# A decoder trunk on one core: the first MLP pair of a block multiplies both input parts in one 512-column matmul, background jobs pause for the residual, two sigmoids move behind an attention split

## The chip, the cores and the metric

The kernel runs on one core of a Trainium2 chip. The metric is the device time of one execution in microseconds (us). Three runs of the kernel before took 1474.15 us in the median (1473.31 to 1476.63). One further execution was profiled.

The engines are written as the profile writes them: PE is the matmul engine, PEld its weight loads, DVE the vector engine, ACT the scalar engine, POOL the GpSimd engine, SP the queue that issues most loads. Each engine works through its own instructions in order.

## The reference, cut to what matters

Two layers on a sequence of 512 tokens, model width 1024, MLP width 4096, all in 32-bit floats:

```python
h = rmsnorm(x, g_mix);  z = h @ w_in            # q, k, v, retention q, k, v, g, two gates
ya = sliding_window_sink_attention(aq, ak, av, sinks) @ w_a
r = chunkwise_retention(rq, rk, rv)             # then a group norm
r = r * rsqrt(mean(r * r) + EPS) * silu(rg);  yb = r @ w_b
x = x + (sigmoid(ga) * ya + sigmoid(gb) * yb) @ w_out
h2 = rmsnorm(x, g_mlp)
x = x + square(relu(h2 @ w_up)) @ w_down        # the MLP
# after both layers: rmsnorm(x, g_final)
```

## The kernel before, in words

**Numbers.** Every operand of a product is split into two parts of a narrower format, high and low: `hi` and `lo` for weights, `xh` and `xl` for inputs. A product is then three matmuls that add up in the same PSUM bank: high by high, high weights by the low input part, low weights by the high input part. The helper `products` (L387 to L396) issues them, on lines L394, L395 and L396. Weights arrive by DMA as tiles of 128 x 1024 called `raw`; `split_until` rounds one on ACT into `hi` (L342) and subtracts on DVE for `lo` (L343), up to three units ahead of PE. `split` (L417, L418) does the same for inputs.

**The MLP.** The 4096 columns of `w_up` go through in eight blocks of 512 a layer. From the second block on (e = 1 to 7) the up-projection of a block is done as two pairs of 256 columns each, by a scheme with seven instead of eight products of half size: tokens in two halves of 256 (`H`), model width in two halves of 512. The sums of inputs that the scheme needs are formed once a layer in `Forms`; the sums of weights are formed in DRAM by background jobs and added on DVE (L283, L306, L322). In `pair` the seven products run as `multiply` calls into three PSUM banks a, e, b; each call takes 4 steps of 128 rows, three matmuls of 256 columns a step. Results are copied or added out of PSUM by ACT and DVE (L1526 to L1546). The first pair of a block hands its result z to `first_two` (or, in the last block of the last layer, `first_plain`), which squares and splits it; the second pair feeds z in pieces to `second`, `second_late` and `second_rest`. `down` then multiplies the squared result by a block of `w_down` in the same scheme: seven `multiply` calls of 12 matmuls with 512 columns. Results go out by POOL DMAs that add into `y` in DRAM (L1674). The framework's scheduler orders instructions across these functions by its own simulated times, so matmuls of `down`, of the first pair and of the second pair interleave on PE.

**Background jobs.** `sum_steps` forms the sums of weights in DRAM: for each job a copying DMA and an accumulating one, both on POOL's queue (L231, L234), the accumulating one behind the copy. In layer 0 there are 27 jobs and a last sum called `sums_last` (L242, L244, L245), so 29 steps; in layer 1 there are 26 jobs and 27 steps. Nothing runs them but calls of `pace(src)`: every second call puts a one-column copy on POOL (L259, `mark`), which waits for `src`, and issues the next step behind it. While `quiet[0]` is set, `pace` does nothing.

**Before the output projection.** The residual x has to leave its place on chip for the gated mixture, which is formed in the same tile (`mixed`). After `w_b` the mixture is turned into input sums on DVE (`ms.first`, `ms.second`, `ms.third`; L1251 to L1267) and split; then POOL loads the residual back, slice by slice (L1307), and the projection `output()` adds its products to it on DVE (L1373 and L1374).

**The retention gate.** `silu(i)` takes a sigmoid on ACT (L1062) and multiplies on DVE (L1063). The first four run after the last exponential of the attention; the last attention output is split on ACT and DVE (L417, L418, into `last_split`), and PE needs that split for `w_a`.

Of the kernel before, what the change touches and what calls it, by code (L numbers as in the profile page):

```python
# [11 lines left out]
F32R = mybir.dt.float32r  # L12
# [104 lines left out]
def decoder(ctx, tc, xT, x_first, w_in, w_rg, w_rv, w_a, w_b, w_wo, w_up, w_pair, w_down, w_end, tables, decay, band, g_last, out):  # L117
# [29 lines left out]
    sink = little_x[:, P - n_gain - n_sink : P - n_gain]  # L147
    eps, half, nsink = (little_x[:, a : a + n] for a, n in ((0, 1), (8, N_KV), (16, n_sink)))
    x = little_x[:, P:].rearrange("p (k t) -> p k t", t=T)
    xh = const.tile([P, KD, T], F32R, name="xh")  # L150
    xl = const.tile([P, KD, T], F32R, name="xl")
    late = ctx.enter_context(tc.tile_pool(name="late", bufs=1))

    def late_tile(dtype):
# [302 lines left out]
    def group(name, layer, moving, evacuates, meanwhile=None, low_last=None):  # L457


        banks = [bank(ps_mm, "mm") for _ in range(4)]  # L460
        for u in range(4):
            with ExitStack() as queue:
                if low_last:
                    state["hold"] = state["next"] + 2 if u < 2 else None
                for ins in behind.pop(0) if behind else ():
                    queue.enter_context(tc.issue_after(ins))
                hi, lo = unit(name, layer)
            if low_last:
                by_halves(
                    banks,  # L470
                    (hi, lo),
                    moving,
                    (2 * u, 2 * u + 1),
                    lambda j, c: slice(j * T + c * P, j * T + (c + 1) * P),
                    low_last.get(u),
                )
            for j in range(0 if low_last else 2):
                advance()
                k = 2 * u + j
                for c, ps in enumerate(banks):  # L480
# [25 lines left out]
    class Forms:  # L506


        def __init__(self, ks):
            self.parts, self.own = {}, []  # L510
            self.tiles = {}
            for k in ks:
                self.tiles[k] = []
                for _ in range(2):
                    t, own = slots.four()
                    self.own.extend(own)
                    self.tiles[k].append([t[:, 2 * i : 2 * i + 2, :].rearrange("p a (b t) -> p (a b) t", t=H) for i in range(2)])

# [3 lines left out]
        def keep(self, ks, first, f, js):  # L522
            hi, lo = self.tiles[ks][first // 2]
            at = slice(2 * (js[0] - first), 2 * (js[-1] - first) + 2)
            split(hi[:, at, :], lo[:, at, :], f[:, at, :])
            for j in js:
                for i in range(2):
                    self.parts[j, ks + i] = tuple(t[:, 2 * (j - first) + i, :] for t in (hi, lo))

        def one(self, ks, b):  # L530
            self.f = [big("sums").rearrange("p a (b t) -> p (a b) t", t=H) for _ in range(2)]
# [89 lines left out]
    def layer_body(layer):  # L621
# [554 lines left out]
        with tc.issue_after(last_exp[0]):  # L1176
            for hs in (slice(0, T // 2), slice(T // 2, T)):
                nc.scalar.activation(x[:, :, hs], x[:, :, hs], AF.Sigmoid)
            for i in range(4):
                silu(i)  # L1180
        turned.take()
        quiet[0] = True
# [43 lines left out]
        class Mixed:  # L1226
# [63 lines left out]

        rT.extend(tuple(view(s) for s in ret[k]) for k in range(4))
        group("w_b", layer, rT, [put_mixed(c) for c in range(4)], {1: second_pair})
        for c in range(6, KD):
            gate_tile(c)
            chunk("w_in", layer, xs, gate(gates[c]))
        for c in range(4, KD):
            quiet[0] = c > 5
            chunk("w_b", layer, rT, put_mixed(c))
        quiet[0] = False
        for k in range(KD):  # L1300
# [181 lines left out]
        def second_late(z):  # L1482
            second(z, TWO, LATE)
            if not kept:
                return
            u_forms.middle(0, kept[0], z, (1,))
            u_forms.keep(0, 2, u_forms.f[1], (2,))

        def second_rest(z):
            if not kept:  # L1490
                return
            kept.pop()
            u_forms.rest(0, z, (3,))
# [15 lines left out]

            return put  # L1510

        def pair(which):
            def multiply(ps, weights, left, moving, start=True):
                hi, lo = weights
                cols = [slice((0 if left else 4 * P) + k * P, (0 if left else 4 * P) + (k + 1) * P) for k in range(4)]
                products(ps, [((hi[:, c], lo[:, c]), m) for c, m in zip(cols, moving)], start, True, not start)

            a, e, b = (bank(ps_mm, "mm")[:, :H] for _ in range(3))
            eu, z = temp("eu"), big("z")
            part = unit("pair", layer)
            multiply(a, part, True, block(0, 0))
            nc.scalar.activation(b, a, AF.Copy)  # L1526
            multiply(e, part, False, sums[0])
            nc.scalar.activation(eu[:, :H], e, AF.Copy)
# [5 lines left out]
            if which:  # L1534
                second(z, slice(0, 1), SOON)
            part = unit("pair", layer)
            multiply(b, part, True, sums[2], False)
            nc.vector.scalar_tensor_tensor(z[:, 1, H:], b, -1.0, eu[:, :H], ALU.mult, ALU.subtract)
            multiply(e, part, False, block(1, 1), False)
            nc.vector.tensor_tensor(z[:, 0, H:], e, eu[:, H:], ALU.add)  # L1540
            nc.scalar.activation(z[:, :, H:], z[:, :, H:], AF.Relu)
            if which:
                second_late(z)
            part = unit("pair", layer)
            multiply(b, part, True, sums[3], False)
            nc.scalar.activation(z[:, 1, :H], b, AF.Relu, scale=-1.0)  # L1546
            if which:
                second(z, slice(1, 2), SOON)
                second_rest(z)
            elif plain:  # L1550
                first_plain(z)
            else:
                first_two(z)

        def down_plain(into):
            sums.free()
# [245 lines left out]
        for e in range(N_BLOCK):  # L1802
            if e == 0:
                into = Adding(e)
                hooks = first_hooks()
                for c in (0, 2):
                    two_chunks("w_up", layer, xs, [put_up(c), put_up(c + 1)], hooks[c // 2])
            else:
                plain = last and e == N_BLOCK - 1
                into = Ending() if e == N_BLOCK - 1 else Adding(e)  # L1810
                if last and e == 2:
                    with tc.issue_after(state["high"]):
                        nc.scalar.activation(sq[:, 0:1], factor[:, 0:1], AF.Sqrt)
                pair(0)
                pair(1)
            if last and e == N_BLOCK - 1:
                down_plain(into)
            else:
                down(e, into, None if e else lambda: rest.append(sum_input(2)))
                if e == 0:  # L1820
                    rest.pop()()
# [185 lines left out]
```

## Time and profile before

| What | Value |
|---|---|
| Median of three runs | 1474.15 us |
| The profiled execution, its own time | 1475.95 us |
| Its span, first to last instruction | 1473.9 us |
| PE busy | 1451.4 us (98%) |
| DVE busy | 1181.1 us (80%) |
| ACT busy | 974.5 us (66%) |
| POOL busy | 229.7 us (16%) |
| Mean granted PE clock | 0.997 |

The profile shows one execution. Rows of the timeline give the start, the duration, the engine, the line and operation, the tile written and those read, the shape, a count where equal instructions are merged, and in brackets the idle time before and who ended it. Matmuls overlap in the pipeline, so the duration of one is longer than the distance to the next. "A <- B: 7.0, 1, 7.0" in the list of waits means that A waited for B for 7.0 us in all, once, and 7.0 us at the longest.

### The profile page before, as it was taken

To read this page: it belongs to the slowest core of one execution; us is meant where nothing else is said; L and a number is where in the kernel's file an instruction comes from. 1 tells how busy PE (TensorE), PEld (TensorE's weight loads), DVE (VectorE), ACT (ScalarE), POOL (GpSimd) and SP (SyncE) were. 2 spreads that over 40 slices of the span, in tenths; PEclk is the share of its full clock that TensorE was granted. 3 is DMA by queue.
4 is the path that set the end of the run, shared out by engine and by line. 5 is a ranking of instruction groups with operands and counts; after the bars stand their busy time and mean duration, and the time that the engine had idled before them with its cause. 6 is when DMAs were issued, how large, how long until landed. Compare 5 with 4: busy or idle time off the path is not lost.

```text
span 1473.9 us, 22472 instructions
## 1 busy us (share of the span) xinstructions
PE 1451.4 (98%) x8185; PEld 1271.8 (86%) x8185; DVE 1181.1 (80%) x1776; ACT 974.5 (66%) x1590; POOL 229.7 (16%) x335
## 2 busy tenths in 40 slices
PE   9999999999899999999999999999999999999998
PEld 7888888888888999999888888888889889999997
DVE  6977877868698888888779788878689888888885
ACT  6656655544487777787656576556447877777775
POOL 0011002321101111111200110022211111111120
PEclk9999999999999999999999999999999999999999
DMA  7598249999735766666964983499975477777664
GB/s 258 180 292 235 90 141 301 285 281 263 201 113 186 182 176 178 180 182 184 313 195 150 288 260 104 151 306 259 280 187 185 154 196 194 191 195 190 175 187 149
DMA packets 97295, 302.83 MB, mean 205 GB/s; under 512 B 11425, under 2 KB 11553, under 8 KB 90785
## 3 DMA queue, kind: packets, MB, share of 16 engines
q0 software_dynamic: 36512, 129.78, 37.5%
q1 hardware_dynamic: 59952, 170.32, 33.9%
q8 instruction: 64, 1.05, 0.3%
q10 hardware_dynamic: 720, 1.31, 0.2%
q14 instruction: 47, 0.38, 0.1%
HBM read 261.78 MB, written 120.06 MB: 259 GB/s over the span
## 4 chain that ended last, share of the span: by engine, by line
PE 90%; DMA 3%; issue 3%; DVE 2%; ACT 1%; POOL 1%; DVEq 0%; POOLq 0%; ACTq 0%
PE mm L395 21%; PE mm L396 21%; PE mm L394 21%; PE wo L1351 4%; PE rg L1015 3%; PE b L394 3%; PE b L395 3%; PE b L396 3%; PE rv L395 2%; PE rv L394 2%; PE rv L396 2%; PE mm L410 2%; DMA sums_up<-w_pair_in 1%; PE score L780 1%; PE pT L745 1%
## 5 line engine op out<-in xcount | busy, mean ns | idle before, releaser
L342 ACT ACTIVATE hi<-raw 128x1024 fp32r<-128x1024 f32 (+1 forms) x393 | 400.1, 1022 | 255.1 <-PE mm L395 120.0
L343 DVE TENSOR_TENSOR lo<-raw,hi 128x1024 fp32r<-128x1024 f32 (+1 forms) x394 | 458.9, 1174 | 93.7 <-ACT hi L342 90.7
L394 PE MATMUL mm<-xh,hi 128*128 128x512 f32 (+1 forms) x912 | 319.1, 354 | 1.7 <-DVE rot L642 0.6
L395 PE MATMUL mm<-xl,hi 128*128 128x512 f32 (+1 forms) x912 | 319.6, 353 | 0.0
L396 PE MATMUL mm<-xh,lo 128*128 128x512 f32 (+1 forms) x912 | 316.2, 353 | 0.1
L394 PEld LDWEIGHTS mm<-xh,hi 128*128 128x128 f32 x912 | 173.2, 190 | 25.7 <-ACT xh L420 1.3
L395 PEld LDWEIGHTS mm<-xl,hi 128*128 128x128 f32 x912 | 173.3, 190 | 21.9
L396 PEld LDWEIGHTS mm<-xh,lo 128*128 128x128 f32 x912 | 172.2, 190 | 21.5 <-DVE lo L343 0.3
L395 PE MATMUL mm<-r,hi 128*128 128x256 f32 (+1 forms) x608 | 189.3, 311 | 0.5 <-DVE r L418 0.5
L394 PE MATMUL mm<-r,hi 128*128 128x256 f32 (+1 forms) x608 | 186.2, 312 | 3.4 <-ACT r L417 2.9
L396 PE MATMUL mm<-r,lo 128*128 128x256 f32 (+1 forms) x608 | 189.0, 311 | 0.0
L394 PEld LDWEIGHTS mm<-r,hi 128*128 128x128 f32 x608 | 115.5, 190 | 12.8 <-ACT r L417 4.0
L395 PEld LDWEIGHTS mm<-r,hi 128*128 128x128 f32 x608 | 115.8, 190 | 9.4 <-DVE r L418 1.4
L396 PEld LDWEIGHTS mm<-r,lo 128*128 128x128 f32 x608 | 115.8, 190 | 6.3
L1674 POOL DMA_DIRECT2D y<-eu x56 | 63.0, 1401 | 372.0 <-DVE eu L1659 371.9
L395 PE MATMUL mm<-lo,r 128*128 128x512 f32 (+1 forms) x276 | 104.3, 387 | 0.0
L396 PE MATMUL mm<-hi,r 128*128 128x512 f32 (+1 forms) x276 | 100.9, 387 | 0.0
L394 PE MATMUL mm<-hi,r 128*128 128x512 f32 (+1 forms) x276 | 98.3, 389 | 0.3 <-ACT r L417 0.2
L394 PE MATMUL b<-hi,r 128*128 128x512 f32 x180 | 70.6, 392 | 1.9 <-DVE eu L1659 1.9
L1351 PE MATMUL wo<-r,hi 128*128 128x256 f32 x384 | 71.0, 287 | 0.0
L283 DVE TENSOR_TENSOR raw<-raw 128x512 f32<-128x512 f32 x56 | 38.5, 687 | 40.5 <-DMA raw<-w_pair_in 32.4
L395 PE MATMUL b<-lo,r 128*128 128x512 f32 x180 | 70.2, 390 | 0.0
(337 smaller groups left out, 2873.0 us busy)
## 6 DMA issues: line engine op xcount, KB each, us to landing
raw<-w_in_in SPq DMA_DIRECT2D x65, 512.0 KB, 5.5
sums_down<-w_down_in POOLq DMA_DIRECT2D x30, 1024.0 KB, 12.8
sums_up<-w_pair_in POOLq DMA_DIRECT2D x56, 512.0 KB, 12.1
raw<-w_down_in SPq DMA_DIRECT2D x45, 512.0 KB, 7.4
raw<-w_pair_in SPq DMA_DIRECT2D x84, 256.0 KB, 3.7
y<-y POOLq DMA_DIRECT2D x62, 256.0 KB, 9.7
y<-eu POOLq DMA_DIRECT2D x61, 256.0 KB, 8.5
raw<-sums_down SPq DMA_DIRECT2D x30, 512.0 KB, 7.2
```

What stands on the lines that cost most here:

```text
L283: nc.vector.tensor_tensor(raws[i][:, at], last[:, LEFT], last[:, RIGHT], ALU.add)
L342: state["high"] = nc.scalar.activation(hi[:, at], raw[:, at], AF.Copy).ins
L343: nc.vector.tensor_tensor(lo[:, at], raw[:, at], f32(hi[:, at]), ALU.subtract)
L394: nc.tensor.matmul(ps, ah, bh, start=start and i == 0, stop=False, **more)
L395: nc.tensor.matmul(ps, ah, bl, start=False, stop=False, **more)
L396: latest[0] = nc.tensor.matmul(ps, al, bh, start=False, stop=stop and i == n - 1, **more).ins
L410: latest[0] = nc.tensor.matmul(ps, w[:, cols(j, c)], moving[k][low], start=first, stop=bool(final)).ins
L745: nc.tensor.transpose(pt[:, i * P : (i + 1) * P], sm[:, at : at + P], ident)
L780: nc.tensor.matmul(ps[:, g * w : (g + 1) * w], q_s[g][:, c, at], part[:, keys], start=i == 0, stop=i == 1)
L1015: nc.tensor.matmul(o, w[:, cols], v, start=start and k == 0 and n == 0 and w is hi and v is vh, stop=k == 3 and n == 1 and w is lo, skip_g ...
L1351: latest[0] = nc.tensor.matmul(o, w[:, cols], v, start=start and first and n % 2 == 0 and w is hi and v is vh, stop=final and w is lo, ski ...
L1674: nc.gpsimd.dma_start(y[:, 2 * j + m, i * T : (i + 1) * T], t, **how)
```

## The change

Three edits.

1. `xh` and `xl` become two halves of one tile `x_both`, and `Forms` also keeps views that hold the high and the low part of a sum together. A new function `wide_pair` does the first pair of each block from e = 1 on: in each step the high weights multiply both input parts in one matmul of 512 columns (two pieces of 256), into both halves of a PSUM bank, and the low weights multiply the high part, 256 columns, into the first half. The halves are added on the way out: by an ACT copy of the first and a DVE operation that adds the second (`joined`), or by two DVE operations. The copy from a to b takes both halves. `pair` keeps the old form and now serves the second pair alone.
2. `quiet[0]` is set before the last two gate chunks (c = 6, 7) instead of in the middle of the last four `w_b` chunks, so that four more calls of `pace` do nothing.
3. `silu(2)` and `silu(3)` are issued after both halves of the last attention split.

```diff
-    xh = const.tile([P, KD, T], F32R, name="xh")
-    xl = const.tile([P, KD, T], F32R, name="xl")
+    x_both = const.tile([P, 2, KD, T], F32R, name="xs")
+    xh, xl = x_both[:, 0], x_both[:, 1]
...
+                    self.both[k].append(t.rearrange("p (c a) (b t) -> p c (a b) t", c=2, t=H))
...
+                    self.wide[j, ks + i] = self.both[ks][first // 2][:, :, 2 * (j - first) + i, :]
...
-            for i in range(4):
+            for i in range(2):
+                silu(i)
+        with tc.issue_after(last_split[0]), tc.issue_after(last_split[1]):
+            for i in range(2, 4):
                 silu(i)
...
+        quiet[0] = True
         for c in range(6, KD):
             gate_tile(c)
             chunk("w_in", layer, xs, gate(gates[c]))
         for c in range(4, KD):
-            quiet[0] = c > 5
             chunk("w_b", layer, rT, put_mixed(c))
         quiet[0] = False
...
+        def wide_pair():
+            def multiply(ps, weights, left, moving, start=True):
+                hi, lo = weights
+                for k, both in enumerate(moving):
+                    at = (0 if left else 4 * P) + k * P
+                    more = {"skip_group_check": True}
+                    nc.tensor.matmul(halves_of(ps), hi[:, at : at + P], both, start=start and k == 0, stop=False, **more)
+                    latest[0] = nc.tensor.matmul(
+                        ps[:, :H], lo[:, at : at + P], both[:, 0, :], start=False, stop=k == 3, **more
+                    ).ins
...
+            def joined(dest, ps, sign=1):
+                nc.scalar.activation(dest, ps[:, :H], AF.Copy, scale=float(sign))
+                nc.vector.scalar_tensor_tensor(dest, ps[:, H:], float(sign), dest, ALU.mult, ALU.add)
+
+            a, e, b = (bank(ps_mm, "mm") for _ in range(3))
+            eu, z = temp("eu"), big("z")
+            part = unit("pair", layer)
+            multiply(a, part, True, quarter_of(0, 0))
+            nc.scalar.activation(b, a, AF.Copy)
+            multiply(e, part, False, form(0))
+            joined(eu[:, :H], e)
+            part = unit("pair", layer)
+            multiply(b, part, True, form(1), False)
+            joined(eu[:, H:], b)
+            multiply(a, part, False, quarter_of(1, 0), False)
+            joined(z[:, 0, :H], a)
+            part = unit("pair", layer)
+            multiply(b, part, True, form(2), False)
+            nc.vector.scalar_tensor_tensor(z[:, 1, H:], b[:, :H], -1.0, eu[:, :H], ALU.mult, ALU.subtract)
+            nc.vector.tensor_tensor(z[:, 1, H:], z[:, 1, H:], b[:, H:], ALU.subtract)
+            multiply(e, part, False, quarter_of(1, 1), False)
+            nc.vector.tensor_tensor(z[:, 0, H:], e[:, :H], eu[:, H:], ALU.add)
+            nc.vector.tensor_tensor(z[:, 0, H:], z[:, 0, H:], e[:, H:], ALU.add)
+            nc.scalar.activation(z[:, :, H:], z[:, :, H:], AF.Relu)
+            part = unit("pair", layer)
+            multiply(b, part, True, form(3), False)
+            joined(z[:, 1, :H], b, -1)
+            nc.scalar.activation(z[:, :, :H], z[:, :, :H], AF.Relu)
+            if plain:
+                first_plain(z)
+            else:
+                first_two(z)
...
-                pair(0)
-                pair(1)
+                wide_pair()
+                pair()
```

More of the change, by code (lines that the diff above doesn't have):

```diff
@@ L510, in __init__ @@
             self.parts, self.own = {}, []
-            self.tiles = {}
+            self.tiles, self.wide, self.both = {}, {}, {}
             for k in ks:
-                self.tiles[k] = []
+                self.tiles[k], self.both[k] = [], []
                 for _ in range(2):
                     t, own = slots.four()
+                    self.both[k].append(t.rearrange("p (c a) (b t) -> p c (a b) t", c=2, t=H))
                     self.own.extend(own)
@@ L1510, in put_up, with halves_of, quarter_of, form @@
             return put
-        def pair(which):
+        def wide_pair():
[8 more added lines that the diff above has]
+                    ).ins
+            def halves_of(ps):
+                return ps.rearrange("p (a t) -> p a t", t=H)
+            def quarter_of(half, tokens):
+                at = slice(tokens * H, tokens * H + H)
+                return [x_both[:, :, k, at] for k in range(4 * half, 4 * half + 4)]
+            def form(j):
+                return [sums.wide[k] for k in sorted(sums.wide) if k[0] == j]
+            def joined(dest, ps, sign=1):
[29 more added lines that the diff above has]
+                first_two(z)
@@ L1513, in multiply, with pair @@
+        def pair():
             def multiply(ps, weights, left, moving, start=True):
@@ L1533, in pair @@
             nc.scalar.activation(z[:, 0, :H], a, AF.Relu)
-            if which:
-                second(z, slice(0, 1), SOON)
+            second(z, slice(0, 1), SOON)
             part = unit("pair", layer)
@@ L1541, in pair @@
             nc.scalar.activation(z[:, :, H:], z[:, :, H:], AF.Relu)
-            if which:
-                second_late(z)
+            second_late(z)
             part = unit("pair", layer)
@@ L1546, in pair @@
             nc.scalar.activation(z[:, 1, :H], b, AF.Relu, scale=-1.0)
[L1547 to L1553, printed above, removed]
+            second(z, slice(1, 2), SOON)
+            second_rest(z)
         def down_plain(into):
```

## The prediction

> **What bounds the kernel now.** I read the page first, then who PE waits for, then three stretches of the timeline.
>
> ```profile
> span 1473.9 us, 22472 instructions
> PE 1451.4 (98%) x8185; PEld 1271.8 (86%) x8185; DVE 1181.1 (80%) x1776; ACT 974.5 (66%) x1590; POOL 229.7 (16%) x335
> ```
>
> PE is busy for 1451.4 of 1473.9 us, so time can come from two places only: fewer or cheaper matmuls, or the 22.5 us in which PE stands. The waits of PE say where it stands:
>
> ```profile
> PE wo L1351 <- DVE lo L343: 7.0, 1, 7.0
> PE mm L394 <- ACT r L417: 3.0, 3, 1.7
> ```
>
> One hole of 7.0 us in the output projection, and short waits of 3.0 us in all behind an attention split. The windows put them beside a steady block of the MLP (columns: stretch, its length, busy us and count of PE, PEld, DVE, ACT, POOL, then PEclk, DMA share, GB/s):
>
> ```profile
> 143.00:182.00 39.00, 37.52 (x192) 31.73 (x191) 33.45 (x46) 23.82 (x34) 1.10 (x2) 1.00 0.30 98
> 380.00:394.00 14.00, 7.30 (x61) 7.10 (x60) 2.30 (x3) 2.72 (x4) 4.08 (x7) 0.93 0.71 188
> 394.00:417.00 23.00, 22.49 (x169) 22.23 (x170) 22.02 (x29) 16.18 (x25) 1.07 (x2) 0.89 0.57 185
> 595.80:635.00 39.20, 39.20 (x253) 35.85 (x252) 32.33 (x42) 30.28 (x50) 7.02 (x8) 1.00 0.70 185
> ```
>
> An MLP block has PE at 39.20 of 39.20, and DVE at 32.33. The change touches all three kinds of place.
>
> **Part 1, the wide pair.** A pair has 7 multiplies of 4 steps, each step three matmuls over 256 columns: 84 matmuls. In the first pair of each of the 14 blocks a step becomes one matmul of 512 and one of 256 columns. What PE pays is the distance between starts, not the duration shown:
>
> ```profile
> 612.12 0.39 PE L394 MATMUL b<-hi,r 128*128 128x512 f32 x1
> ...
> 614.84 0.28 PE L394 MATMUL mm<-xh,hi 128*128 128x256 f32 x1
> ...
> 616.27 0.40 PE L394 MATMUL b<-hi,r 128*128 128x512 f32 x1
> ```
>
> Twelve 512-column matmuls fill 612.12 to 614.84, 226.7 ns each; twelve of 256 fill 614.84 to 616.27, 119.2 ns each. A block is 168 x 119.2 + 84 x 226.7 ns = 39.07 us, against 39.20 in the window, so the two prices carry the stage. A step falls from 3 x 119.2 = 357.6 to 226.7 + 119.2 = 345.9 ns: 11.7 ns. There are 28 steps a pair and 14 pairs: 392 x 11.7 ns = 4.6 us. No row shows a moving operand in two pieces of 256 columns that lie apart. Its bounds: no gain, if each piece costs what a matmul of 256 costs (2 x 119.2 = 238.4 ns, as now); 4.6 us, if it costs what a 512-column row costs. A loss is excluded as long as one instruction with one weight load is not dearer than the two it replaces. I take 4.6: within a piece the columns lie side by side, as in the 512-column rows, and doubling the columns there costs 107.5 ns where a matmul of 256 costs 119.2, so 11.7 ns belong to the instruction and not to the columns.
>
> The Trainium skill ("TensorE: Matmul & The Clock Gate", section "Back-to-back issue gap") gives an isolated gap of N/2.4 + 2.5 ns, 109 and 216 ns here; by it a step would gain 2.6 ns and the part 1.0 us instead of 4.6. The trace disagrees with these gaps by about 10 ns a matmul (119.2 and 226.7), and the page itself says that a stream with a weight load before each matmul is not set by that formula.
>
> What the pair adds lies on ACT and DVE:
>
> ```profile
> L1538 DVE SCALAR_TENSOR_TENSOR z<-mm,eu 128x256 f32<-128x256 f32 x28 | 11.8, 420 | 10.1 <-PE mm L396 10.1
> L1612 ACT ACTIVATE b<-mm 128x512 f32<-128x512 f32 x30 | 17.5, 584 | 4.8 <-PE mm L396 4.8
> L1541 ACT ACTIVATE z<-z 128x512 f32<-128x512 f32 x28 | 17.3, 619 | 0.6 <-DVE z L1540 0.6
> 629.76 0.37 ACT L1546 ACTIVATE z<-mm 128x256 f32<-128x256 f32 x1
> ```
>
> DVE had 2 evacuations, now 8: six more of 0.42, 2.5 us a block; 32.33 becomes 34.8 of 38.9 us, still with room. ACT: the copy of a to b grows from 0.37 to 0.58, and one more Relu over 512 costs 0.62: 0.8 us on 30.28. I cost both at nothing, since PE is what these engines wait for in this stage (the L1538 row: 10.1 us idle before it, all on PE). If that cover is gone, it is 2.5 us a block, 35 us in all.
>
> The order matters more than the sums. The result of the first pair now goes Copy, DVE add, Relu, where it was one Relu: later by 0.42 + (0.62 - 0.37) = 0.7 us and a hand-over. Who waits for it is the next block-product:
>
> ```profile
> 632.33 0.62 ACT L417 ACTIVATE r<-z 128x512 fp32r<-128x512 f32 x1
> 633.34 0.69 DVE L418 TENSOR_TENSOR r<-z,r 128x512 fp32r<-128x512 f32 x1
> 634.85 0.63 PE L394 MATMUL mm<-hi,r 128*128 128x512 f32 x2
> 636.74 0.40 PE L395 MATMUL mm<-lo,r 128*128 128x512 f32 x1
> ```
>
> The high part is ready at 632.95 and used at 634.85, the low at 634.03 and used at 636.74: 1.9 and 2.7 us of room for about 1 us. It holds. Bank b is tighter: it is written again one multiply (4 x 345.9 ns = 1.4 us) after ACT and DVE start to read it; that is the slower rival below.
>
> **Part 2, the pause.** The hole, followed on PE, DVE, POOL and in the chain of work:
>
> ```profile
> 394.35 0.58 PE L1351 MATMUL wo<-r,lo 128*128 128x256 f32 x1 [7.05 <-DVE lo L343]
> ...
> 398.57 0.58 PE L1351 MATMUL wo<-r,hi 128*128 128x256 f32 x2
> ```
> ```profile
> 362.11 0.68 DVE L1267 SCALAR_TENSOR_TENSOR x<-x 128x512 f32<-128x512 f32 x1
> 377.75 0.68 DVE L1267 SCALAR_TENSOR_TENSOR x<-x 128x512 f32<-128x512 f32 x1
> 392.47 0.69 DVE L1373 TENSOR_TENSOR x<-x,kept 128x512 f32<-128x512 f32 x1 [11.70 <-DMA x<-xT_in]
> ```
> ```profile
> 360.02 0.83 POOL L234 DMA_DIRECT2D sums_down<-w_down_in  x1 [4.53 <-DMA sums_down<-w_down_in]
> 360.56 0.60 POOL L259 COPY mark<-gb 128x1 f32<-128x1 f32 x1
> 370.69 1.08 POOL L244 DMA_DIRECT2D sums_last<-sums_down  x1 [9.53 <-issue]
> 381.48 0.83 POOL L245 DMA_DIRECT2D sums_last<-w_down_in  x1 [9.72 <-DMA sums_last<-sums_down]
> 382.12 3.44 POOL L1307 DMA_DIRECT2D x<-xT_in  x6
> ```
> ```profile
> 383.77 8.62 DMA x<-xT_in
> ```
>
> POOL issues in order. The mark from gate chunk 7 (L259 at 360.56) sets off the last job step, two accumulating DMAs that each wait for the one before, and the loads of x stand behind them until 382.12. DVE then waits 11.70 us for x, the weight split L343 stands behind that, and PE 7.05 us behind the split. PE restarts slowly too: 19 matmuls from 394.35 to 398.57 take 4.22 us where 119.2 ns each make 2.26, so 1.96 more (the clock column reads 0.93 and 0.89). The hole costs 9.0 us.
>
> Counting calls of pace in layer 0 (8 in attention, 8 and 6 for the gates, 2 and 4 in qk, 8 in values, 16 in retention, 4 in the group): 56 before gate chunk 6, so 28 steps; the list needs 29. The pause takes away the four calls of chunks 6 and 7 and of two w_b chunks, and with them exactly that last step, which comes two calls later, in the projection's own put, after the loads of x. Then POOL is free from about 361, the first two slices of x go when L1267 at 362.11 has ended and the others from 378.4, when the second L1267 has. With the 8.62 us that such a load took, the slices for the first L1373 are there before 375, those for the second at 387 at the latest; it ran 4.6 us after the first, at about 385. A wait of 2 us there is inside the room DVE has: PE lost only 7.05 of DVE's 11.70. The last step lands later, but nothing queued on POOL wants to go until the first y store:
>
> ```profile
> 454.75 1.11 POOL L1674 DMA_DIRECT2D y<-y  x2 [58.40 <-ACT y L1669]
> ```
>
> I take 9.0; it is 5 if the second pair of slices comes late enough to hold DVE. Layer 1 has no such wait in the list, and its 27 steps end before the pause: nothing there.
>
> **Part 3, two sigmoids.** In both layers PE waits for the last attention split:
>
> ```profile
> 148.57 1.15 ACT L1062 ACTIVATE sig<-z 128x512 f32<-128x512 f32 x2
> 149.74 0.60 ACT L638 ACTIVATE rot<-mm 64x512 f32<-64x512 f32 x1
> ```
> ```profile
> 152.60 1.19 PE L394 MATMUL mm<-r,hi 128*128 128x512 f32 x4 [1.21 <-ACT r L417]
> 154.06 0.50 PE L395 MATMUL mm<-r,hi 128*128 128x512 f32 x1 [0.27 <-DVE r L418]
> ```
>
> The two sigmoids, 1.15 us, stand on ACT ahead of the split; behind it, the split comes 1.15 us sooner, and so does PE until it meets the low half on DVE. Bounds: 0, if another wait takes over, and 1.21 + 0.27 = 1.5 a layer. I take 1.0, as the low half has its own queue: 2.0 us in all. Queued behind the moved sigmoids on ACT is the preparation of the turned inputs (L895), and behind their two products on DVE its subtractions. PE wants these only after w_a and the first gate product; where they come too late for it, part 3 falls towards its lower bound.
>
> **The sum.** 4.6 + 9.0 + 2.0 = 15.6 us off the profiled execution's own time, 1475.95 us (its span is 1473.9, 2.05 less): 1460.35. The median of the runs, 1474.15, is 1.8 below that execution, so 1458.6 is what I predict.
>
> **Rivals.** (A) The wide matmul brings nothing, because the two pieces are read as two: parts 2 and 3 remain, 11.0 us, 1463.2. For it: no row shows such an operand. Against: the 11.7 ns that two matmuls of 256 cost more than one of 512. By the isolated gap of that page of the Trainium skill it would be 1462, nearly this case. (B) The pause does not fill the hole, as the later slices of x, freed only at 378.4, are late by their 8.62 us and hold DVE: part 2 is worth 5, or, with the throttled restart kept, 3; 1463 to 1465. This is the case in which the change does not do what it says. For it: 387 against 385. Against: PE's 4.6 us of room. (C) Slower: bank b. After its second and third product ACT (0.37) and DVE (0.42) must both have read it, and each may first have to finish a split already begun:
>
> ```profile
> L343 DVE TENSOR_TENSOR lo<-raw,hi 128x1024 fp32r<-128x1024 f32 x360 | 436.6, 1220 | 77.6 <-ACT hi L342 74.6 <-PE mm L395 1.5
> L342 ACT ACTIVATE hi<-raw 128x1024 fp32r<-128x1024 f32 x360 | 379.4, 1058 | 243.8 <-PE mm L395 119.5 <-issue 22.0 <-PE rv L396 21.4
> ```
>
> 0.37 + 0.42 + 1.06 + 1.22 = 3.1 us against the 1.4 us of the multiply between, a stall of 1.7 a block, 24 us in 14 blocks: 1482 after the gains. It decides from 15.6/14 = 1.1 us a block; at just that, the result is no change. Against it: matmuls of other products stand between in the trace (b forms between two multiplies at 616.27), and ACT and DVE idle for PE here, not PE for them.
>
> **How the numbers follow.** Forecast 0.66, (A) 0.13, (B) 0.07, (C) in full 0.10, a stall that just cancels the gains 0.04. The forecast's own spread is 1455 (both bounds of part 3, every end at its best: 4.6 + 9.0 + 3.0, and 2 us for the run) to 1463; A and B reach 1467 with a little more lost. So 1455 to 1467 leaves out C, the cancelling case and little else. Faster by over 0.2% (3 us, about what a measurement of this kernel can tell): 0.86; within: 0.04; slower: 0.10.
>
> **What would show it.** Right: a block of about 38.9 us with PE at 100%; matmuls of 512 in the first pair 227 ns apart from the next; no wait of wo L1351 on DVE, L1307 ahead of L244, no PEclk below 1.0 there; the wait on ACT r L417 near zero in both layers. Wrong: new waits of PE on ACT or DVE evacuations inside the MLP blocks, blocks of 40 us or more, or a hole that merely moved behind L1373.

## The result, and the profile after

The changed kernel takes 1517.8 us (median of 4 runs, 1517.37 to 1518.16) against 1474.44 us of the kernel before (4 runs beside it). The ratio is 1.0292, 95% interval 1.0274 to 1.031: slower by 43 us, where 16 us less was forecast. The profiled execution took 1518.16 us, its span is 1516.4 us.

The page first: the span, and busy time, share and instructions of each engine.

```profile
span 1516.4 us, 21805 instructions
PE 1461.0 (96%) x7793; PEld 1251.3 (83%) x7793; DVE 1210.9 (80%) x1860; ACT 980.0 (65%) x1604; POOL 227.2 (15%) x335
```

PE issues 392 matmuls fewer (7793 against 8185), exactly one a step, and yet is busy longer, and it stands for 55.4 us where it stood for 22.5. The waits of PE (total, times, longest) name the places:

```profile
PE mm L394 <- ACT r L417: 21.2, 14, 2.7
PE mm L1523 <- DVE eu L1540: 13.8, 12, 1.2
PE mm L396 <- DVE lo L343: 4.0, 2, 3.7
PE ret L394 <- DVE whole L770: 1.9, 1, 1.9
```

Two waits stand in nearly every MLP block. The 7.0 us of the output projection are gone. The windows of the changed kernel, in the columns of the prediction's windows; the last row is three blocks:

```profile
380.00:394.00 14.00, 14.00 (x119) 14.00 (x118) 11.87 (x15) 6.73 (x8) 3.17 (x4) 1.00 0.91 289
394.00:417.00 23.00, 22.84 (x142) 20.46 (x141) 22.14 (x34) 19.91 (x33) 0.83 (x1) 1.00 0.74 192
510.54:638.51 127.97, 120.28 (x672) 103.32 (x672) 102.86 (x142) 92.47 (x151) 21.06 (x24) 1.00 0.66 173
```

A block is 127.97/3 = 42.66 us long, 3.4 more than the 39.2 of before, and no engine is full in it: PE is busy for 40.1 us, DVE for 34.3, ACT for 30.8. That every engine has idle time points to the hand-overs between them rather than to a load; the experiments test it. Fourteen blocks of 3.4 would make 48 us; the output projection gives 9 back.

**The first wait, once a block.** The timeline of PE, ACT and DVE around it:

```profile
591.20 0.28 PE L1524 MATMUL mm<-r,lo 128*128 128x256 f32 x1
...
594.92 0.28 PE L396 MATMUL mm<-xs,lo 128*128 128x256 f32 x1
596.52 0.50 PE L394 MATMUL mm<-hi,r 128*128 128x512 f32 x1 [1.33 <-ACT r L417]
596.86 0.39 PE L395 MATMUL mm<-lo,r 128*128 128x512 f32 x1
...
591.40 1.06 ACT L342 ACTIVATE hi<-raw 128x1024 fp32r<-128x1024 f32 x1 [1.38 <-PE mm L1523]
592.37 0.37 ACT L1539 ACTIVATE z<-mm 128x256 f32<-128x256 f32 x1
...
594.09 0.63 ACT L1565 ACTIVATE z<-z 128x512 f32<-128x512 f32 x1 [0.41 <-DVE z L1540]
594.75 1.06 ACT L1471 ACTIVATE z<-z 128x1024 f32<-128x1024 f32 x1
595.84 0.63 ACT L417 ACTIVATE r<-z 128x512 fp32r<-128x512 f32 x1
...
592.49 1.23 DVE L343 TENSOR_TENSOR lo<-raw,hi 128x1024 fp32r<-128x1024 f32 x1 [2.29 <-ACT hi L342]
593.64 0.42 DVE L1540 SCALAR_TENSOR_TENSOR z<-mm,z 128x256 f32<-128x256 f32 x1
```

The last product of the first pair ends on PE with the L1524 of 591.20. Its result is copied by ACT only at 592.37, behind a weight split begun just before; DVE adds the second half only at 593.64, behind the other half of that split; then come Relu, Square and the split into r. PE gets r 5.2 us after its next matmul could start (591.32 to 596.52). It has 31 matmuls of the second pair to do meanwhile, to 595.04, and then stands.

**The second wait, once a block.** The same three engines, 28 us later:

```profile
621.57 0.40 PE L394 MATMUL b<-hi,r 128*128 128x512 f32 x1
...
623.21 0.28 PE L1524 MATMUL mm<-xs,lo 128*128 128x256 f32 x1
624.65 0.50 PE L1523 MATMUL mm<-xs,hi 128*128 128x512 f32 x1 [1.16 <-DVE eu L1540]
...
623.17 0.69 ACT L1721 ACTIVATE y<-b,columns 128x512 f32<-128x512 f32 x1 [3.35 <-PE b L396]
623.76 0.38 ACT L1539 ACTIVATE eu<-mm 128x256 f32<-128x256 f32 x1
...
624.17 0.42 DVE L1540 SCALAR_TENSOR_TENSOR eu<-mm,eu 128x256 f32<-128x256 f32 x1 [3.62 <-ACT eu L1539]
```

PE wants to write bank e again at 623.33, and e has been complete since 619.1. But its copy to eu (L1539) stands on ACT behind the evacuation of the block-product before (L1721), ACT has stood idle for 3.35 us for that one, and the six matmuls that L1721 waits for begin on PE only at 621.57, put by the scheduler between the third and the fourth step of the pair's fourth product. So PE waits for DVE, DVE for ACT, and ACT for matmuls that PE itself took late.

**The other two parts** did their work. POOL and DVE in layer 0 of the changed kernel:

```profile
362.46 1.16 POOL L1312 DMA_DIRECT2D x<-xT_in  x2 [8.15 <-DVE r L418]
...
380.38 1.06 POOL L1312 DMA_DIRECT2D x<-xT_in  x2 [2.41 <-DVE r L418]
...
389.31 1.11 POOL L244 DMA_DIRECT2D sums_last<-sums_down  x1
...
377.66 0.69 DVE L1378 TENSOR_TENSOR x<-x,kept 128x512 f32<-128x512 f32 x1
```

The loads of x go ahead of the last job step, DVE takes x at 377.66 without a wait (at 392.47 after 11.70 us before), and PE is full from 380 to 394 at a granted clock of 1.00.

### The profile page after: what moved, and what is told of

It reads as the page before. It is cut to its first block, busy times and chain, and to the rows that moved or that the text cites. A ratio compares the mean times of both kernels' runs of the same rounds, so it can differ in the third digit from the quotient of the medians.

```text
span 1516.4 us, 21805 instructions
## 1 busy us (share of the span) xinstructions
PE 1461.0 (96%) x7793; PEld 1251.3 (83%) x7793; DVE 1210.9 (80%) x1860; ACT 980.0 (65%) x1604; POOL 227.2 (15%) x335
## 4 chain that ended last, share of the span: by engine, by line
PE 88%; ACT 5%; issue 3%; DVE 3%; DMA 1%; ACTq 0%; DVEq 0%
PE mm L394 18%; PE mm L395 18%; PE mm L396 17%; PE mm L1523 6%; PE wo L1356 5%; PE mm L1524 3%; PE rg L1017 3%; PE b L394 2%; PE b L395 2%; PE b L396 2%; ACT hi L342 2%; PE rv L395 2%; PE rv L394 2%; PE rv L396 2%; PE mm L410 1%
## 5 line engine op out<-in xcount | busy, mean ns | idle before, releaser
L343 DVE TENSOR_TENSOR lo<-raw,hi 128x1024 fp32r<-128x1024 f32 (+1 forms) x394 | 461.2, 1176 | 113.4 <-ACT hi L342 98.6
L396 PE MATMUL mm<-xs,lo 128*128 128x512 f32 (+1 forms) x744 | 271.7, 370 | 4.0 <-DVE lo L343 4.0
L394 PE MATMUL mm<-xs,hi 128*128 128x512 f32 (+1 forms) x744 | 271.3, 368 | 2.3 <-DVE z L997 1.0
L395 PE MATMUL mm<-xs,hi 128*128 128x512 f32 (+1 forms) x744 | 271.4, 367 | 0.0
L396 PEld LDWEIGHTS mm<-xs,lo 128*128 128x128 f32 x744 | 140.4, 189 | 26.7 <-DVE lo L343 4.4
L394 PEld LDWEIGHTS mm<-xs,hi 128*128 128x128 f32 x744 | 140.3, 189 | 25.4 <-ACT xs L420 1.4
L395 PEld LDWEIGHTS mm<-xs,hi 128*128 128x128 f32 x744 | 140.3, 189 | 21.3
L394 PE MATMUL mm<-hi,r 128*128 128x512 f32 (+1 forms) x276 | 106.9, 394 | 21.2 <-ACT r L417 21.2
L395 PE MATMUL mm<-r,hi 128*128 128x256 f32 (+1 forms) x384 | 126.1, 330 | 0.4 <-DVE r L418 0.4
L396 PE MATMUL mm<-r,lo 128*128 128x256 f32 (+1 forms) x384 | 125.8, 329 | 0.0
L394 PE MATMUL mm<-r,hi 128*128 128x256 f32 (+1 forms) x384 | 122.6, 332 | 0.4 <-DVE z L1596 0.4
L1523 PE MATMUL mm<-r,hi 128*128 128x512 f32 x224 | 80.7, 397 | 0.0
L394 PEld LDWEIGHTS mm<-r,hi 128*128 128x128 f32 x384 | 72.4, 191 | 9.3 <-ACT r L417 1.0
L394 PEld LDWEIGHTS mm<-hi,r 128*128 128x128 f32 x276 | 52.1, 189 | 33.6 <-ACT r L417 24.1
L1523 PE MATMUL mm<-xs,hi 128*128 128x512 f32 x168 | 66.1, 419 | 14.2 <-DVE eu L1540 13.8
L395 PEld LDWEIGHTS mm<-r,hi 128*128 128x128 f32 x384 | 73.1, 190 | 8.0 <-DVE r L418 0.8
## 6 DMA issues: line engine op xcount, KB each, us to landing
sums_up<-w_pair_in POOLq DMA_DIRECT2D x56, 512.0 KB, 11.7
```

Source lines behind the costliest of these rows:

```text
L343: nc.vector.tensor_tensor(lo[:, at], raw[:, at], f32(hi[:, at]), ALU.subtract)
L394: nc.tensor.matmul(ps, ah, bh, start=start and i == 0, stop=False, **more)
L395: nc.tensor.matmul(ps, ah, bl, start=False, stop=False, **more)
L396: latest[0] = nc.tensor.matmul(ps, al, bh, start=False, stop=stop and i == n - 1, **more).ins
L1523: nc.tensor.matmul(halves_of(ps), hi[:, at : at + P], both, start=start and k == 0, stop=False, **more)
```

## The experiments

Three theories at first. **E**: the loss is the way in which the first pair's results leave PSUM, ACT and DVE one after the other. **M**: it is the matmul of two pieces itself. **O**: the pause or the sigmoids cost time elsewhere. Ratios are to the kernel before on the same chip (medians 1475.19 and 1475.47 us), with 95% intervals.

**The parts by themselves.** Three kernels from the one before: both small parts, the pause alone, the sigmoids alone.

```diff
-            for i in range(4):
+            for i in range(2):
                 silu(i)
+        with tc.issue_after(last_split[0]), tc.issue_after(last_split[1]):
+            for i in range(2, 4):
+                silu(i)
...
+        quiet[0] = True
         for c in range(6, KD):
...
-            quiet[0] = c > 5
```

> The kernel before with the pause and the two moved sigmoids, both MLP pairs in the old form (part 1 undone). Theory E (the whole loss comes from the way in which the first pair's results leave PSUM): parts 2 and 3 keep their worth, 9.3 us for the hole in the output projection and 1 to 3 us for the sigmoids, so 1462 to 1464 us, blocks of the MLP back at 39.2 us. Rival M (the loss comes from the 512-column matmul in two pieces): the same number, this run does not tell E from M. Rival O (the pause and the sigmoids cost time elsewhere, in layer 1 above all, where the score stretch was longer): 1470 us or more.

Measured: 1463.91 us, 0.9925 (0.9912 to 0.9938). O falls. This is also the best version that was found and beats both kernels by a measured margin.

> The kernel before with the pause alone (part 2). By the prediction it is worth 9.0 us: 1465 to 1467 us, no wait of PE in the output projection of layer 0. Rival: the loads of x still come late for half of it, 1469 to 1471 us.

Measured: 1466.58 us, 0.9943 (0.993 to 0.9957): 8.6 us, where 9.0 were forecast.

> The kernel before with the two moved sigmoids alone (part 3). By the prediction 1.0 us a layer: 1472 to 1473.5 us. Rival: another wait takes over in both layers, 1474 to 1476 us.

Measured: 1471.72 us, 0.9977 (0.9968 to 0.9986): 3.5 us where 2.0 were forecast. PE at the attention split of layer 1 in the kernel before, whose layer 0 the prediction shows, and in this run in both layers:

```profile
886.88 1.19 PE L394 MATMUL mm<-r,hi 128*128 128x512 f32 x4 [1.65 <-ACT r L417]
888.34 0.50 PE L395 MATMUL mm<-r,hi 128*128 128x512 f32 x1 [0.27 <-DVE r L418]
```
```profile
153.10 0.49 PE L395 MATMUL mm<-r,hi 128*128 128x512 f32 x1 [0.38 <-DVE r L418]
...
885.03 0.51 PE L395 MATMUL mm<-r,hi 128*128 128x512 f32 x1 [0.38 <-DVE r L418]
```

The wait on ACT is gone in both layers, and a shorter one on DVE is left. By the times of PE on either side of the two splits, they give 1.1 and 1.5 us. The rest lies in the hole of the output projection, which this run still has: PE waits 6.5 us there instead of 7.0 and restarts sooner. Next to the pause the sigmoids add 1466.58 - 1463.91 = 2.7 us.

The wide pair alone, the changed kernel with those two parts undone:

> The wide first pair alone, the pause and the sigmoids as in the kernel before. Theories E and M: blocks of 42.7 us as in the changed kernel, 14 x 3.4 = 48 us over the kernel before, and the hole of 7 us in the output projection is back: 1522 to 1530 us. Rival O: nearer to 1500 us, the pause or the sigmoids having a share in the long blocks.

Measured: 1529.13 us, 1.0375 (1.0358 to 1.0391). Part 1 costs 54 us by itself, and the same 54 us (1517.8 - 1463.9) on top of the others. So no interplay of part 1 with the other two is to be seen.

**The matmul or the way out.** First the matmuls narrow again, the way out as changed:

```diff
-    nc.tensor.matmul(halves_of(ps), hi[:, at : at + P], both, start=start and k == 0, ...)
+    for half in range(2):
+        nc.tensor.matmul(ps[:, half * H : half * H + H], hi[:, at : at + P], both[:, half, :], start=start and k == 0, ...)
```

In this kernel both matmuls that open a bank carry the start flag, which changes the result.

> The changed kernel with each 512-column matmul of the wide pair split into two of 256 columns, into the same two halves of the bank: the matmuls are those of the kernel before, the way out (copy and add, each half by itself) is that of the changed kernel. Theory E: the loss stays, blocks of 42.7 us or more, 1518 us plus at most 4.6 us for the dearer steps: 1515 to 1523 us. Rival M: the loss goes, 1462 to 1468 us.

Measured: 1503.3 us, 1.0197 (1.0183 to 1.0212). Both expectations missed. M is far off: with narrow matmuls the first wait is still there.

```profile
PE mm L394 <- ACT r L417: 19.3, 13, 3.2
```

E's number missed by 12 us. In this trace the scheduler has put the last block-product ahead of the pair's fourth product, and the second wait is down to 0.3 us; a run below makes just that edit. Then the other way round, wide matmuls and the old way out:

```diff
-    nc.scalar.activation(dest, ps[:, :H], AF.Copy, scale=float(sign))
-    nc.vector.scalar_tensor_tensor(dest, ps[:, H:], float(sign), dest, ALU.mult, ALU.add)
+    nc.scalar.activation(dest, ps[:, :H], func, scale=float(sign))   # Copy for eu, Relu for z
...
-    nc.vector.tensor_tensor(z[:, 1, H:], z[:, 1, H:], b[:, H:], ALU.subtract)
-    nc.vector.tensor_tensor(z[:, 0, H:], z[:, 0, H:], e[:, H:], ALU.add)
```

> The changed kernel with the wide matmuls kept, and the second half of each bank left in PSUM: the result leaves out the product of the high weights with the low input part in the first pair, and every result leaves by one instruction as in the kernel before. Theory E: PE no longer waits, blocks of 38.9 us and the forecast's price of the wide matmul comes true: 1457 to 1462 us. Rival M: blocks stay over 41 us, 1500 us or more.

Measured: 1463.35 us, 0.9921 (0.9907 to 0.9935). The loss of 54 us is gone with the matmuls still wide: E holds, M falls. Four blocks in the windows of this run, and four of the run with both small parts and no wide pair:

```profile
504.10:660.05 155.95, 155.95 (x899) 137.53 (x898) 129.42 (x165) 122.32 (x197) 27.91 (x32) 1.00 0.70 190
```
```profile
504.56:661.57 157.01, 157.01 (x1011) 143.59 (x1009) 129.49 (x165) 121.36 (x198) 27.98 (x32) 1.00 0.70 188
```

PE is full in both: 38.99 against 39.25 us a block, 0.26 us or 9.5 ns a step. The wide matmul is worth 14 x 0.26 = 3.7 us where its way out costs nothing. In this run only 0.6 us of it reached the end (1463.91 against 1463.35, less than the spread of the runs): the waits of PE name 2.2 us on ACT eu L1583 and 1.9 us on DVE whole L770 that the run without a wide pair does not have.

**Each wait by itself.** One edge in the order of PE:

```diff
+    down_last = latest[0]
...
-    multiply(a, part, False, quarter_of(1, 0), False)
+    with tc.issue_after(down_last):
+        multiply(a, part, False, quarter_of(1, 0), False)
```

> The changed kernel with one edge in the order of PE: the first pair's fourth product does not begin before the last product of the block-product of the block before has been issued; the changed kernel had put three of its four steps ahead. Theory Q (the wait of L1523 on eu comes from the order alone: the copy of e stands on ACT behind the copy of that last product): 13.8 us of waits on eu and their slow restarts go, the wait on r stays at 21 us, blocks of 41.4 to 41.6 us, 1501 to 1506 us. Rival: eu is late for another reason (weight splits ahead of the copy), no change, 1515 us or more.

Measured: 1500.75 us, 1.017 (1.0154 to 1.0186), 17 us less. Among the waits the one on eu L1540 is gone, the first stays:

```profile
PE mm L394 <- ACT r L417: 18.5, 13, 2.6
```

So with this way out the second wait comes from the scheduler's order; that the copy on ACT has its share in it too is shown by the reduction below. This is 2.5 us below the run with the narrow matmuls, where the fourth product also stands behind that block-product and the way out is the same: about the worth of the wide matmul. Then one instruction in place of three at the end of the chain:

```diff
-    joined(z[:, 1, :H], b, -1)
-    nc.scalar.activation(z[:, :, :H], z[:, :, :H], AF.Relu)
+    nc.scalar.activation(z[:, 0, :H], z[:, 0, :H], AF.Relu)
+    nc.scalar.activation(z[:, 1, :H], b[:, :H], AF.Relu, scale=-1.0)
```

> The changed kernel with only the last result of the first pair leaving by one instruction, Relu of the first half of its bank: the result leaves out the high weights' product with the low input part in that quarter. Theory H: the wait of PE on r (21.2 us) goes with its slow restarts, the wait on eu (13.8 us) stays, blocks of 41.1 to 41.4 us, 1494 to 1499 us. Rival C (the wait is there because less work of the second pair is left behind the last product, not because its way out is longer): half of the wait on r or more stays, 1506 us or more.

Measured: 1503.3 us, 1.0186 (1.0169 to 1.0204): 14.5 us less where 19 to 24 were expected, and in neither range. The waits:

```profile
PE mm L1523 <- DVE eu L1540: 12.6, 12, 1.1
PE mm L394 <- DVE z L1596: 6.3, 12, 0.5
```

The wait on r fell from 21.2 to 0.2 us, so the longer way out is its cause in this order; but another stood right behind it, on a bank of the second pair that DVE reads late (L1596), and took part of the gain.

**Order and way out together.** How many matmuls of the second pair lie behind the first pair's last product can be counted in the order of PE's instructions: 48 in the kernel before (5.7 us at 119.2 ns) and in the run with the old way out, 31 in the changed kernel (3.7 us), each in nearly every block. They are the cover, the work that PE has while the result is on its way. With the narrow matmuls and the changed way out it is 31 too: the cover goes with the way out and not with the wide matmul. The next kernel restores the 48 in the changed kernel, by the edge above and one more:

```diff
     multiply(b, part, True, form(3), False)
+    wide_last[:] = [latest[0]]
...
-    multiply(b, part, True, sums[1], False)          # in pair()
+    with tc.issue_after(wide_last[0]):
+        multiply(b, part, True, sums[1], False)
```

> The changed kernel with two edges in the order of PE and nothing else: the first pair's fourth product behind the last product of the block before, and the second pair's third product behind the first pair's last one, so that 48 matmuls of 256 columns (5.7 us) are left to cover the way of the first result to the next block-product, where the changed kernel leaves 31 (3.6 us). Theory K (both waits are the order's: the longer way out fits in if PE has enough other work behind it): no wait on r or eu over 0.3 us a block, blocks of 39.4 to 39.8 us, 1466 to 1473 us. Rival H (the longer way out costs wherever it stands): another wait on DVE or ACT takes their place, blocks over 40.5 us, 1483 us or more.

Measured: 1492.24 us, 1.0118 (1.0101 to 1.0135). Both old waits are gone, and a new one is there, on the second pair's evacuation; the waits, and DVE ahead of it:

```profile
PE mm L394 <- DVE z L1602: 15.9, 14, 1.3
```
```profile
630.21 1.22 DVE L306 TENSOR_TENSOR raw<-raw 128x1024 f32<-128x1024 f32 x1
631.34 1.22 DVE L343 TENSOR_TENSOR lo<-raw,hi 128x1024 fp32r<-128x1024 f32 x1
632.64 0.69 DVE L534 TENSOR_TENSOR sums<-z 128x512 f32<-128x512 f32 x1
633.25 0.42 DVE L1602 SCALAR_TENSOR_TENSOR z<-mm,eu 128x256 f32<-128x256 f32 x1
```

The blocks are about 41 us long. So K falls and H holds for this way out: it is too long for both orders tried. DVE works without a gap from 628.73 up to L1602, and the add of the first result (0.42 us at 629.87) is part of that queue; how much of the new wait each of its parts makes was not told apart. The other lever is the way out alone: one DVE reduction that adds the two halves, with no ACT in between. The Relu then goes to each half of z as it is ready, so that the last one takes 256 columns instead of 512; what each of the two does was not told apart.

```diff
 def joined(dest, ps):
-    nc.scalar.activation(dest, ps[:, :H], AF.Copy, scale=float(sign))
-    nc.vector.scalar_tensor_tensor(dest, ps[:, H:], float(sign), dest, ALU.mult, ALU.add)
+    nc.vector.tensor_reduce(dest, ps.rearrange("p (a t) -> p t a", t=H), mybir.AxisListType.X, ALU.add)
```

> The changed kernel with the two halves of a bank joined by one DVE reduction over the pair of halves (512 in, 256 out) where it was an ACT copy and a DVE add; Relu goes to each half of z as it is ready. Theory H (the loss is the hand-over: a result crosses the queues of ACT and DVE one after the other, each time behind other work): both waits of PE go or fall below 0.3 us a block, blocks of 38.9 to 39.4 us, 1458 to 1466 us. Rival L (the loss is the added load on DVE, 34 us of a block): DVE carries as much or more, blocks stay over 41 us, 1495 us or more.

Measured: 1487.58 us, 1.0085 (1.0071 to 1.0099), 30 us less than the changed kernel, between the two ranges. Its waits, then the busy line of its page, and the reduction on DVE beside PE at the place of the second wait:

```profile
PE mm L394 <- ACT r L417: 8.9, 12, 0.9
PE mm L394 <- DVE z L1596: 4.7, 13, 1.2
PE mm L1523 <- DVE eu L1539: 3.7, 2, 3.0
```
```profile
PE 1454.2 (98%) x7793; PEld 1246.3 (84%) x7793; DVE 1220.8 (82%) x1860; ACT 968.4 (65%) x1562; POOL 229.5 (15%) x335
```
```profile
613.87 1.28 DVE L1539 TENSOR_REDUCE eu<-mm 128x256 f32<-128x512 f32 x2
...
613.98 0.39 PE L394 MATMUL b<-hi,r 128*128 128x512 f32 x1
```

DVE carries more than in the changed kernel (1220.8 us against 1210.9) and the kernel is 2% faster, so the load, L, does not explain the loss, though L had the length of most blocks right: eight are 41.2 us long. The next run carries still more on DVE (1223.7 us) in shorter blocks. The wait on eu is left twice. In the block of the last two rows the six matmuls of the block-product (from 613.98) still stand inside the fourth product, but DVE has begun to empty the banks at 613.87, not behind ACT's copy of that block-product. The second wait thus needed both, the order and the copy on ACT. The cover is not restored: 26 matmuls in those eight blocks, 31 in three. With the reduction and the second of the two edges:

> The kernel with one DVE reduction for each join, and the second pair's third product put behind the first pair's last one, as in the run beside it. Theory K: the wait on r (0.7 us a block) and the one on z (0.4 us) go, blocks of 39.2 to 39.8 us, 1462 to 1472 us. Rival H: 1483 us or more.

Measured: 1470.06 us, 0.9966 (0.9954 to 0.9979): K holds here, with blocks of 39.6 us in the mean and a cover that alternates between 48 and 36 matmuls. The wide pair with its full result is faster than the kernel before, though 6 us behind the kernel without it. What remains among its waits:

```profile
PE mm L1525 <- DVE eu L1541: 3.6, 2, 3.1
PE mm L394 <- DVE z L1600: 2.1, 6, 0.4
```

Side by side, the four medians are: changed order and way out 1517.8; order mended 1492.2; way out mended 1487.6; both 1470.1. Alone the two mend 26 and 30 us, together 48 of the 54. The two are not quite apart: with the reduction the scheduler moved the matmuls again (26 instead of 31), and the last kernel has only one of the two edges.

## Why the prediction was wrong

**The step that failed** is in part 1: "I cost both at nothing, since PE is what these engines wait for in this stage", and then "1.9 and 2.7 us of room for about 1 us. It holds." The load that the first sentence has in mind was not what cost the time: with the reduction DVE carries 40 us more than before, and with one edge added the kernel is faster than before. What failed is the room. The forecast of 1458.6 us and its range (1455 to 1467) were given as if the order on PE would stay as the trace of before showed it. Three things in it were off.

- *The room.* The 1.9 us were there because 48 matmuls of the second pair lay behind the last product. The changed kernel has 31 there: 17 x 119.2 ns, 2.0 us of cover, went with the edit. The text before the prediction says that the scheduler orders across functions by its own simulated times; the prediction held the old order for given.
- *The length.* The sum "0.42 + (0.62 - 0.37) = 0.7 us and a hand-over" leaves the Copy out: Copy, add and Relu in place of one Relu are 0.37 + 0.42 + 0.62 - 0.37 = 1.04 us, and two hand-overs more. From the copy to the split of z it is 2.57 us before (629.76 to 632.33) and 3.47 after (592.37 to 595.84). That this 0.9 is near the forecast's 1 us is luck. The add alone waits 0.9 us behind a weight split already begun (592.74 to 593.64, L343), which was not costed; but two instructions that stood between Square and split in the kernel before are not there after:

```profile
631.12 1.04 ACT L342 ACTIVATE hi<-raw 128x1024 fp32r<-128x1024 f32 x1
632.07 0.36 ACT L1528 ACTIVATE eu<-mm 128x256 f32<-128x256 f32 x1
```

The rows of the weight splits were in the prediction, but used for bank b alone. Room of 1.9 us became a stop of 1.5 us (595.04 to 596.52), 3.4 us apart: 2.0 of them are the lost cover, the other 1.4 the longer way out, 0.9 from the copy to the split and most of the rest ahead of the copy. It starts 1.17 us behind the start of the last matmul (591.20 to 592.37) instead of 0.79 (628.97 to 629.76).

- *The second wait* was not foreseen in any form: a copy behind an evacuation that waits for a later matmul. It took the new order and a copy on ACT: one edge removed it, and the reduction left it in two blocks.

Rival C had the right sign and half of the mechanism, new reads of PSUM behind splits already begun, and the wrong place: not bank b, but the last result and bank e, at 3.4 us a block instead of 1.7. It got 0.10, on the ground that ACT and DVE idle for PE here. That idle time is spread over the block; the 3.47 us from the copy to the split it did not shorten.

**What held.** The price of the wide matmul: with no wait in the way a block took 38.99 us where 38.9 was forecast, and 9.5 ns a step instead of 11.7; the bound "no gain, if each piece costs what a matmul of 256 costs" is excluded. Rival A is thereby wrong. The gap formula of the Trainium skill ("TensorE: Matmul & The Clock Gate", section "Back-to-back issue gap") would give an estimate of 2.5 ns a step (2.6 in the prediction). The measured 9.5 is far from it, as the page lets one expect for a stream with a weight load before each matmul. The pause: 8.6 us for 9.0, the loads of x ahead of the last job step, no second wait at L1378; rival B is wrong. The sigmoids: 3.5 us alone and 2.7 next to the pause, for 2.0. Layer 0 gave the 1.0 that was forecast (1.1); layer 1 had 1.65 + 0.27 us to give where layer 0, from whose rows the bound was taken, had 1.48, and gave 1.5. Without part 1 the same sum gives 1474.15 - 9.0 - 2.0 = 1463.2, and the run took 1463.9; that it is so near owes something to the two misses going opposite ways.

**What stays open.** The 48 us are three steady blocks times fourteen, not a measured sum. At the same places of the two traces, the changed kernel is 2.4 us ahead of the run without a wide pair when PE reaches the sums of squares before the MLP of layer 0 (423.00 against 425.36; a difference of the first 25 us, where no block has run). It is 25.5 behind at those before the MLP of layer 1 (1179.32 against 1153.86) and 53.8 behind at the end. So the MLP of layer 1 loses 28.3 us, seven times 3.4 and about 4 more, and the MLP of layer 0 with the attention of layer 1 loses 27.8, again about 4 more. Beside the two waits there lie in these stretches stops on L343 (4.0 us) and L770 (1.9), and three stretches of 3.4 us in which the granted clock is 0.50 (from 725.3, 899.4 and 1213.4), where the run without a wide pair shows 1.00 throughout. Which part of the new order makes these stops was not tried.

## What to carry to other kernels

Idle time of an engine did not pay for added work here, because that work stands in a chain on which the bound engine waits. Add up the chain from the last matmul to its consumer, each hop behind the longest instruction that may have begun, and compare it with the matmuls that lie in between. Where a scheduler sets the order, an edit changes that order too, so the cover must be counted in the changed kernel's instructions and not in the old trace. A saving of 10 ns on each of many matmuls (3.7 us here) was outweighed here by a longer chain of hand-overs that repeats in every block.

## What the hardware showed beyond that

The cost of a stop is not the stop alone. After the stops of 1.2 to 1.3 us in the blocks the first matmul lost a little: 0.34 us from 596.52 to 596.86, where 0.23 is the price; no slower clock followed. After a stop of 3.08 us, in the run with both levers, PE and then the windows show:

```profile
1185.39 0.50 PE L1525 MATMUL mm<-xs,hi 128*128 128x512 f32 x1 [3.08 <-DVE eu L1541]
...
1186.53 0.57 PE L1525 MATMUL mm<-xs,hi 128*128 128x512 f32 x1
...
1187.11 0.41 PE L394 MATMUL mm<-xs,hi 128*128 128x256 f32 x1
...
1189.46 0.41 PE L396 MATMUL mm<-xs,lo 128*128 128x256 f32 x1
```
```profile
1185.40:1190.00 4.60, 4.60 (x21) 4.38 (x22) 4.15 (x6) 0.51 (x2) 0.00 (x0) 0.63 1.09 293
```

Three wide steps ran at the usual price, but for 0.1 us on the first matmul (1.14 us from 1185.39 to 1186.53), and then twelve matmuls of 256 columns came 214 ns apart instead of 119 (eleven distances from 1187.11 to 1189.46). The granted clock of the whole stretch is 0.63, and from 1187.10 to 1189.60 alone it is 0.50. PE was slow not at once behind the stop but a microsecond later, while it was full.

The length of the stop does not decide this. With the reduction alone PE stands 3.03 us for the same eu (to 1193.40), and the granted clock stays at 1.00 from 1193.40 to 1205. In the changed kernel a stop of 1.93 us (to 897.87) is followed by 0.53 from 899.20 to 902.80. The Trainium skill ("TensorE: Matmul & The Clock Gate", section "Part 1: The HAM clock gate (the "warmup" mystery)") has the clock halved after an idle window of about 3.4 us. The half agrees with the 0.50 here; both stops that it followed are shorter than that window, and what decides between 3.08 and 3.03 us these runs do not show.
